# GLU contraction in two parts between the S5 steps, the last norm weight on ScalarE, S5 tables asked for eight slots later

## The chip, the cores and the metric

One core of one Trainium2 chip runs the whole kernel. The metric is the device time of one launch in microseconds; the kernel before takes 2509.47 us (median of three runs, 2509.09 to 2511.0).

## What is computed

One inference step of a two-layer decoder trunk, for a prompt of 256 tokens and for 8 samples of 4 new tokens each, with the same weights in float32. The first layer mixes with retention and a gated linear recurrence; the second with an S5 state space model whose output goes through a GELU and a GLU; each layer ends in a SwiGLU feed-forward network (FFN), and the trunk ends in a norm.

```python
D_MODEL = 2048
FFN_HIDDEN = 5632          # 44 tiles of 128
def odd_mixer(x, h0_re, h0_im, g, ..., w_glu, b_glu):
    u = rmsnorm(x, g)
    y, hr, hi = s5(u, h0_re, h0_im, ...)    # 128 groups of 16 channels, 64 complex states each
    y = jax.nn.gelu(y)
    z = y @ w_glu + b_glu                   # 2048 x 4096
    z1, z2 = jnp.split(z, 2, axis=-1)
    return z1 * jax.nn.sigmoid(z2), hr, hi
def swiglu(x, w_gu, w_down):
    g, u = jnp.split(x @ w_gu, 2, axis=-1)
    return (jax.nn.silu(g) * u) @ w_down
def trunk(x, ...):
    for layer in range(2):
        out = even_mixer(x, ...) if layer == 0 else odd_mixer(x, ...)
        x = x + out
        x = x + swiglu(rmsnorm(x, norm_ffn[layer]), ...)
    return rmsnorm(x, norm_final), states
```

## The kernel before

**Layout.** Channels lie on the 128 partitions (16 tiles of a 2048-wide vector, NT = 16) and the tokens on N = 288 columns: four S5 time steps of 72 columns, each 8 sample columns and 64 chunk columns. The trunk's value is `X` (128 x 16 x 288) in SBUF.

**Main matmuls.** A weight tile of 128 x 128 is used as a high and a low part, and so is the input: three matmuls of 288 columns for each tile, L314 (weight high, input high), L315 (weight high, input low) and L316 (weight low, input high). A *unit* is one tile of 128 output rows over a run of k-tiles. `halves_of` cuts a unit into two *slots* of weights, up to eight k-tiles or 1024 columns wide. Each slot goes through three steps: SyncE asks for its DMA (`raw`, L262, 512 KB, four buffers), ScalarE copies out the high part (`wh`, L268, four buffers), VectorE subtracts it for the low part (`wl`, in `tt` at L96, three buffers, and a fourth, `wlx`, from FFN0 on).

**What sets the order.** `run_prog` goes through the list `prog` item by item. Ahead of each item it issues DMAs for slots until four are ahead of the last subtracted one, copies until four are ahead of the last finished slot, and subtractions until three are (four while `hold` has an entry). `later(n, f)` puts `f` behind the n-th slot from now; `bgq` holds background work that runs behind slots. Each engine takes its instructions in the order in which they were issued, and SyncE's DMA queue (SPq) carries the weights, the S5 tables and the rows of X that S5 needs.

**The stages.** Even mixer (`w_in`, `w_out`); FFN0 (`w_gu`, `w_dn`, the 44 hidden tiles in thirds of 15, 15 and 14), in whose background `table_chunk` builds the S5 tables P, R, O and T into DRAM, through the DMA queue of GpSimd (POOL); `s5_open`, which asks for the S5 state `ss` and the first tables; `s5_core` and the S5 steps with the GLU among them; the other GLU units, in pairs of a z unit and a g unit for each of 16 output tiles; FFN1; `finish`, the last norm and the output.

**An S5 step** treats one tile of 128 channels: `st_a` multiplies the input by the norm and by table P (L1426, 32 small matmuls into `pp`); `st_b1` turns it by the table R on VectorE; `st_t` is a direct part with the table T (L1476, 16 small matmuls into `po`); `st_b2` runs two scans (L1451) and turns back, ending in the state `Hs`; `st_o` multiplies the state by the table O (L1486, 32 small matmuls into `po`); `st_d1`, `st_d1b`, `st_d2` and `st_d3` are the GELU and the split of its output. In a step j before, the GELU of groups j-2, j-3 and j-4 is under way (`st_d1(j-2)` to `st_d3(j-4)`), so that 20 steps are needed for 16 groups. Tables are double-buffered: `load("P", j + 2)`, `load("R", j + 1)`, `load("T", j + 1)` and `load("O", j)` at the head of `stage_a`. P, R and O are 512 KB each; T is put together by four strided DMAs into a tile that was zeroed once.

**GLU in the S5 steps.** Units 0 and 1 get one k-tile each, six matmuls in all, in each of the steps 4 to 19. Unit 2 gets its two halves behind steps 17 and 19. This is 144 of the GLU's 1536 matmuls; the other 29 units follow.

**The end.** Behind each FFN1 output tile `final_hook` squares it on ScalarE and adds it up on VectorE. `finish` sums over partitions with a matmul by ones, takes Ln and Exp on ScalarE for the reciprocal root and refines it, and then makes 16 products of 288 columns (`stt` at L105, X times weight times root), each with a DMA of its own.

Of the kernel before, what the change touches and what calls it, by code (L numbers as in the profile page):

```python
# [19 lines left out]
P = 128  # L20
# [26 lines left out]
def trunk_kernel(ctx: ExitStack, tc: tile.TileContext, ins, outs, upto=99, dbg=None):  # L47
# [6 lines left out]
    xgp = ctx.enter_context(tc.tile_pool(name="xgp", bufs=32))  # L54
# [16 lines left out]
    def xg_(dt=F32R):  # L71
        return xgp.tile([P, N], dt, tag="x", name=nm("xg"))

# [144 lines left out]
    def run_prog():  # L218
        ws, items, hold, fin_h = [], [], [], set()
        own = None  # L220
        lead = [u for u in prog if isinstance(u, Unit)][:4]
        for u in prog:
            if isinstance(u, Unit):
# [3 lines left out]
                for e in range(2):  # L227
                    for h in hs:
                        items.append((len(ws),) + h[e])
                        ws.append(h[e])  # L230
            elif isinstance(u, tuple):
                us, stages = u
                hs = [halves_of(x) for x in us]
                idx = {}
                for x, e in ((0, 0), (1, 0), (0, 1), (1, 1), (2, 0), (2, 1)):
                    idx[x, e] = len(ws)
                    ws.append(hs[x][e])
                items.append(lambda h=idx[2, 0]: hold.append(h))
                own = us[2]
                for a, segs, b, free in stages:  # L240
                    items.append(a)
                    for x, k0, k1 in segs:
                        items.append((idx[x, k0 >= hs[x][0][2]], us[x], k0, k1))
                    items.append(b)
                    if free:
                        items.append(hold.clear)
            else:
                items.append(u)
        accs = {}
        raws, whs, wls = {}, {}, {}  # L250
        n = len(ws)
        LH, RAW = 3, 4
        ring = S["ring"] = [wt.tile([P, 1024], F32R, name=f"wl{k}", bufs=1) for k in range(3)]
        free = S["free"] = list(ring)

        def size(i):
            return (ws[i][2] - ws[i][1]) * P

        def dma(i):
            u, a, b = ws[i]  # L260
            r = wt.tile([P, 1024], F32, tag="raw", name=nm("raw"), bufs=RAW)
            sp.dma_start(r[:, :size(i)], u.w[:, a * P:b * P])  # L262
            raws[i] = r

        def prep_h(i):
            w = size(i)
# [4 lines left out]
        def prep_l(i):  # L271
            w = size(i)
# [20 lines left out]
        for h in items:  # L293
            while True:
# [4 lines left out]
                if c[2] >= done + (4 if hold else 3) or c[2] >= n or c[2] in hold:  # L299
# [5 lines left out]
            i, u, a, b = h  # L305
            if a == u.k0:
                bank = mp_() if u in lead else S["bank"]() if u is own else psa.tile([P, 512], F32, tag="acc", name=nm("acc"))
                accs[id(u)] = (bank[:, :N], u.rhs())
            acc, rhs = accs[id(u)]
            wh, wl, w0 = whs[i], wls[i], ws[i][1]  # L310
# [1464 lines left out]
```

## Time and profile before

| | |
|---|---|
| runs | 2511.0, 2509.09, 2509.47 us (median 2509.47) |
| profiled execution | 2510.14 us, its span 2508.4 us |
| TensorE matmul (PE) | 2440.5 us busy, 97% |
| VectorE (DVE) | 1631.0 us busy, 65% |
| ScalarE (ACT) | 1126.3 us busy, 45% |
| GpSimd (POOL) | 113.6 us busy, 5% |
| DMA | 485.38 MB, 194 GB/s mean |
| chain that ended last | PE 93%, DVE 4%, DMA 2%, issue 1% |

Times are microseconds from the start of the span. The S5 steps lie from 1344 to 1455 us, the GLU's pairs from there to 1648 us, FFN1 to 2492 us. In the rows, a number in square brackets is the idle time of that engine just before the instruction, and behind the arrow stands what ended it; a line that is a helper's (L96 is every `tt`, L105 every `stt`) is told apart by the tile's name.

### The profile page before, as it was taken

Reading aid. Unit: us, or ns where it says so; the run is one execution under the profiler, and the core shown is the slowest. Engines: PE = TensorE matmul, PEld = TensorE weight load, DVE = VectorE, ACT = ScalarE, POOL = GpSimd, SP = SyncE. Lnnn points to the kernel's source line nnn. Section 1 sums busy time; section 2 is a strip of 40 time slices with the busy share of each in tenths; the row PEclk is TensorE's granted clock in tenths of the full one; section 3 lists DMA queues with packets and bytes.
Section 4 is the critical chain, followed back from the end, with each engine's and each line's share of the span. In section 5 each row is a group of like instructions: output and inputs, shape, how many; then the busy total and the mean of one; then the engine's idle time right before and its main releaser. Section 6 shows DMA issues by size and latency. Waiting matters only on the chain.

```text
span 2508.4 us, 49325 instructions
## 1 busy us (share of the span) xinstructions
PE 2440.5 (97%) x20090; PEld 2410.8 (96%) x20090; DVE 1631.0 (65%) x3011; ACT 1126.3 (45%) x1692; POOL 113.6 (5%) x221
## 2 busy tenths in 40 slices
PE   8999999999999999999997799999999999999997
PEld 8999999999999999999996689999999999999997
DVE  7767676667777887777847975555544555445554
ACT  6655554433455555455532444443333333333342
POOL 0111110000011011101100000000000000000000
PEclk9999999999999999999999899999999999999999
DMA  7555655555577778777788945555555555555553
GB/s 249 193 188 185 208 169 173 176 163 166 177 254 239 237 239 260 242 233 244 229 241 255 270 149 166 166 162 167 168 166 171 159 163 163 174 163 163 163 162 126
DMA packets 170371, 485.38 MB, mean 194 GB/s; under 512 B 35744, under 2 KB 52000, under 8 KB 170144
## 3 DMA queue, kind: packets, MB, share of 16 engines
q1 hardware_dynamic: 155792, 437.94, 55.6%
q0 software_dynamic: 12624, 42.95, 4.9%
q8 instruction: 158, 2.59, 0.4%
q10 hardware_dynamic: 1728, 1.33, 0.2%
q14 instruction: 69, 0.57, 0.1%
HBM read 440.77 MB, written 41.37 MB: 192 GB/s over the span
## 4 chain that ended last, share of the span: by engine, by line
PE 93%; DVE 4%; DMA 2%; issue 1%; ACT 0%; SPq 0%; DVEq 0%; POOL 0%; ACTq 0%; POOLq 0%
PE acc L314 30%; PE acc L316 29%; PE acc L315 29%; DVE w L96 2%; DVE w L1451 1%; DMA raw<-in_w_dn_dram 0%; PE mp L774 0%; DVE Hs L96 0%; PE mp L519 0%; DMA tab<-tabR 0%; DVE g L105 0%; PE mp L1297 0%; PE mp L315 0%; DMA tab<-tabP 0%; PE mp L316 0%
## 5 line engine op out<-in xcount | busy, mean ns | idle before, releaser
L314 PE MATMUL acc<-xg,wh 128*128 128x288 f32 x3520 | 1045.1, 297 | 0.0
L268 ACT ACTIVATE wh<-raw 128x1024 fp32r<-128x1024 f32 (+1 forms) x736 | 757.2, 1035 | 444.3 <-PE acc L315 297.3
L316 PE MATMUL acc<-xg,wl 128*128 128x288 f32 x2816 | 827.6, 294 | 0.8 <-DVE wl L96 0.8
L315 PE MATMUL acc<-xg,wh 128*128 128x288 f32 x2608 | 766.5, 294 | 1.6 <-DVE xg L105 1.6
L96 DVE TENSOR_TENSOR wl<-raw,wh 128x1024 fp32r<-128x1024 f32 (+1 forms) x585 | 692.8, 1197 | 37.3 <-ACT wh L268 29.6
L314 PEld LDWEIGHTS acc<-xg,wh 128*128 128x128 f32 x3520 | 660.3, 188 | 1.8 <-issue 0.8
L314 PE MATMUL acc<-ac,wh 128*128 128x288 f32 x2064 | 612.4, 297 | 4.5 <-ACT wh L268 2.2
L316 PEld LDWEIGHTS acc<-xg,wl 128*128 128x128 f32 x2816 | 529.7, 188 | 1.0 <-DVE wl L96 1.0
L315 PEld LDWEIGHTS acc<-xg,wh 128*128 128x128 f32 x2608 | 491.5, 188 | 2.5 <-DVE xg L105 2.0
L316 PE MATMUL acc<-ac,wl 128*128 128x288 f32 x1592 | 469.2, 295 | 1.3 <-DVE wl L96 1.3
L315 PE MATMUL acc<-ac,wh 128*128 128x288 f32 x1568 | 461.4, 294 | 0.0
L315 PE MATMUL acc<-x,wh 128*128 128x288 f32 x1408 | 415.4, 295 | 0.0
L314 PEld LDWEIGHTS acc<-ac,wh 128*128 128x128 f32 x2064 | 389.0, 188 | 7.0 <-ACT wh L268 2.5
L96 DVE TENSOR_TENSOR g<-acc,rstd 128x288 f32<-128x288 f32 x192 | 87.6, 457 | 341.4 <-PE acc L316 341.3
L316 PEld LDWEIGHTS acc<-ac,wl 128*128 128x128 f32 x1592 | 300.8, 189 | 1.5 <-DVE wl L96 1.5
L315 PEld LDWEIGHTS acc<-ac,wh 128*128 128x128 f32 x1568 | 295.9, 189 | 0.0
L315 PEld LDWEIGHTS acc<-x,wh 128*128 128x128 f32 x1408 | 264.2, 188 | 0.1
L316 PE MATMUL acc<-xg,wlx 128*128 128x288 f32 x704 | 206.8, 294 | 0.0
L96 DVE TENSOR_TENSOR X<-X,acc 128x288 f32<-128x288 f32 x112 | 50.9, 454 | 233.9 <-PE acc L316 233.6
L96 DVE TENSOR_TENSOR wlx<-raw,wh 128x1024 fp32r<-128x1024 f32 (+1 forms) x151 | 179.5, 1189 | 2.6 <-ACT wh L268 2.6
L191 ACT ACTIVATE ac<-g 128x288 fp32r<-128x288 f32 x98 | 43.5, 444 | 282.7 <-DVE g L96 282.7
L316 PE MATMUL acc<-ac,wlx 128*128 128x288 f32 x472 | 138.8, 294 | 0.0
(288 smaller groups left out, 2003.3 us busy)
## 6 DMA issues: line engine op xcount, KB each, us to landing
raw<-in_w_gu_dram SPq DMA_DIRECT2D x352, 512.0 KB, 4.6
raw<-in_w_dn_dram SPq DMA_DIRECT2D x128, 448.0 KB, 4.2
raw<-in_w_in_dram SPq DMA_DIRECT2D x96, 512.0 KB, 4.6
raw<-in_w_dn_dram SPq DMA_DIRECT2D x64, 512.0 KB, 3.7
raw<-in_w_glu_dram SPq DMA_DIRECT2D x64, 512.0 KB, 5.0
raw<-in_w_out_dram SPq DMA_DIRECT2D x32, 512.0 KB, 4.3
out_ret_s_dram<-s POOLq DMA_DIRECT2D x16, 512.0 KB, 5.6
pw<-tabW SPq DMA_DIRECT2D x128, 64.0 KB, 3.8
```

The source lines that it names most:

```text
L96: v.tensor_tensor(o, a, b, op=op)
L191: act.activation(h, x, AF.Copy, scale=scale)
L268: act.activation(wh[:, :w], raws[i][:, :w], AF.Copy)
L314: pe.matmul(acc, lhsT=wh[:, o:o + P], rhs=xh, start=(k == u.k0), stop=False)
L315: pe.matmul(acc, lhsT=wh[:, o:o + P], rhs=xl, start=False, stop=False)
L316: pe.matmul(acc, lhsT=wl[:, o:o + P], rhs=xh, start=False, stop=(k == u.k1 - 1))
L1451: v.tensor_tensor_scan(g[:, ri].rearrange("p q c -> p (q c)"), r4m, a[:, ri].rearrange("p q c -> p (q c)"), 0.0, op0=MUL, op1=ADD)
```

## The change

It has six parts.

1. The GLU is contracted in two parts. The first part of 28 of the 32 units (g0 to g11 over k-tiles 0 to 3, two units sharing a slot of 1024 columns; g12, g13 and z0 to z13 over k-tiles 0 to 5, in slots of 768) stands between the S5 steps: one k-tile of g0 and g1 each in the steps 2 to 5, two more units behind step 5, three behind steps 6 and 7, two behind each of the steps 8 to 16. These are 432 matmuls. ScalarE copies each part from PSUM to SBUF; the later unit over the remaining 10 or 12 k-tiles adds it (in the same `stt` for z, with one more `tt` for g). The unit 2 with its own PSUM bank and `hold` are gone. Units of the tiles 14 and 15 stay whole.
2. A step j now does the GELU of group j-1 from end to end, `st_o(j - 1)` stands at its head, and 17 steps do. The tables are asked for in other places of the step, P and O and T one step earlier.
3. T is put together in DRAM during FFN0 (`tabU` to `tabT`, zero-filled first, ten more POOL DMAs for each two groups) and loaded by one DMA of 256 KB.
4. `s5_open` runs eight slots later, and asks for `ss`, P0, R0, T0, P1, O0, R1, T1, O1 instead of `ss`, P0, P1, R0, T0.
5. S5's norm sum is four matmuls into 32 rows each, with one `ts` behind it instead of four; the matmuls that keep TensorE busy at S5's start are others.
6. The last norm's weight is multiplied into X on ScalarE behind each FFN1 output tile. `finish` takes the last tile's square into the matmul by ones directly, loads the ScalarE table ahead of time, and makes six products (576 to 1152 columns) with six DMAs.

```diff
@@ run_prog
-                us, stages = u
-                for x, e in ((0, 0), (1, 0), (0, 1), (1, 1), (2, 0), (2, 1)):
...
+                for pieces in u[0]:
+                    slot(*pieces)
+                items.extend(u[1])
...
-                if c[2] >= done + (4 if hold else 3) or c[2] >= n or c[2] in hold:
+                if c[2] >= done + 3 or c[2] >= n:
@@ final_hook
+    def last_hook(j):
+        if j == 0:
+            S["fb"] = cst.tile([P, N], F32, tag="nacc", name=nm("nacc"))
+        if j < NT - 1:
+            norm_acc(S["fb"], j, X[:, j, :])
+        else:
+            S["sq"] = g_()
+            act.activation(S["sq"], X[:, j, :], AF.Square)
+        act.activation(X[:, j, :], X[:, j, :], AF.Copy, scale=vec[:, V_FIN + j:V_FIN + j + 1])
@@ ffn, rest, table_chunk
-                call(lambda: act.activation(lnw, eps, AF.Ln))
+                call(lambda: act.preload_act_table_set("natural_log_exp_and_others"))
...
-        bgq.append(s5_open)
+        bgq.append(lambda: later(8, s5_open))
...
+            for jj in range(2):
+                pool.dma_start(tabT[2 * ch + jj].rearrange("p q c -> p (q c)"), ins["zero"])
...
-                pool.dma_start(tabT[j], T)
+                pool.dma_start(tabU[j], T)
...
+                for s in range(CH):
+                    pool.dma_start(tabT[j, 32 * s:32 * s + 32, :, 32 * s:], src[:, :, :P - 32 * s])
@@ s5_open
-        for k, j in (("P", 0), ("P", 1), ("R", 0), ("T", 0)):
+        for k, j in (("P", 0), ("R", 0), ("T", 0), ("P", 1), ("O", 0), ("R", 1), ("T", 1), ("O", 1)):
@@ s5_core
         def stage_a(j):
-            load("P", j + 2)
-            load("R", j + 1)
-            load("T", j + 1)
-            load("O", j)
-            if 0 <= j - 2 < NT:
-                st_d1(j - 2)
+            if j:
+                load("R", j + 1)
+                st_o(j - 1)
+                load("O", j + 1)
+                st_d1(j - 1)
             if j + 1 < NT:
                 st_a(j + 1)
...
+                load("P", j + 3)
             if j < NT:
                 st_b1(j)
                 st_t(j)
+                load("T", j + 2)
@@ glu
+        def first(key, w, k1, alloc):
+            def ev(ps):
+                part[key] = alloc()
+                act.activation(part[key], ps, AF.Copy)
+            cut[key] = k1
+            return Unit(w, 0, k1, lambda: xs["y"], ev)
+
+        g1 = [first(("g", j), ins["w_glu"][NT + j], 4 if j < 12 else 6, lambda: ac_(F32)) for j in range(NT - 2)]
+        g1 += [first(("z", j), ins["w_glu"][j], 6, lambda: xg_(F32)) for j in range(NT - 2)]
+        slots = [[(u, 0, 4) for u in g1[2 * i:2 * i + 2]] for i in range(6)] + [[(u, 0, 6)] for u in g1[12:]]
+        todo = deque(g1[2:])
+        seq = []
+        for t in range(NT + 1):
+            seq.append(lambda t=t: (S["a"](t), S["b"](t)))
+            if 2 <= t < 6:
+                seq += [(u, t - 2, t - 1) for u in g1[:2]]
+            for _ in range(0 if t < 5 else {6: 3, 7: 3}.get(t, 2)):
+                u = todo.popleft()
+                seq.append((u, 0, u.k1))
...
+                if ("g", j) in part:
+                    src = t_
+                    tt(t_, ps, part.pop(("g", j)), ADD)
...
-            segs = [(x, t - 4, t - 3) for x in range(2) if t >= 4]
@@ finish
-        norm_finish(acc, rstd["v"])
-        for j in range(NT):
-            y = g_()
-            stt(y, X[:, j, :], vec[:, V_FIN + j:V_FIN + j + 1], rstd["v"], MUL, MUL)
-            (sp if j % 2 else act).dma_start(outs["y"][:, j, :], y)
+        pe.matmul(ps[:, :N], lhsT=ones, rhs=S["fb"], start=True, stop=False)
+        pe.matmul(ps[:, :N], lhsT=ones, rhs=S["sq"], start=False, stop=True)
...
+        for q, a, b in ((sp, 0, 2), (act, 2, 5), (sp, 5, 9), (act, 9, 13), (sp, 13, 15), (act, 15, 16)):
+            y = X[:, a:b, :]
+            tt(y, y, r[:, None, :].to_broadcast([P, b - a, N]), MUL)
+            q.dma_start(outs["y"][:, a:b, :], y)
```

On VectorE, in one S5 step of the second half (`Hs` is the end of a step's state, the `w` rows the turns by table R, `g`, `xg` and `xl` the GELU). Before:

```order
L105 SCALAR_TENSOR_TENSOR g_16719<-g_16804,g_16718 128x288
L96 TENSOR_TENSOR Hs_16499<-w_16843,w_16904 128x8x64
L96 TENSOR_TENSOR xg_15937<-xg_15937,r4n 128x288
L96 TENSOR_TENSOR w_16949<-pp_16826,tab_16812 128x512
L96 TENSOR_TENSOR w_16950<-pp_16826,tab_16812 128x512
L105 SCALAR_TENSOR_TENSOR xg_16912<-g_16719,ac_16911 128x288
L96 TENSOR_TENSOR w_16949<-w_16949,w_16950 128x512
```

and with the change:

```order
L108 SCALAR_TENSOR_TENSOR g_17976<-g_18031,g_17975 128x288
L99 TENSOR_TENSOR Hs_16587<-w_18000,w_18029 128x8x64
L108 SCALAR_TENSOR_TENSOR xl_18037<-g_17976,ac_18036 128x288
L99 TENSOR_TENSOR wlx<-raw_17644,wh_17934 128x768
L99 TENSOR_TENSOR wl_119<-raw_17782,wh_18063 128x768
L99 TENSOR_TENSOR xg_16464<-xg_16464,r4n 128x288
L99 TENSOR_TENSOR w_18155<-pp_17981,tab_17939 128x512
L99 TENSOR_TENSOR w_18156<-pp_17981,tab_17939 128x512
L99 TENSOR_TENSOR w_18155<-w_18155,w_18156 128x512
```

Two subtractions of 768 columns have come in between one step's `Hs` and the next step's first turn, and the GELU's last product now stands behind `Hs` instead of among the turns.

On SyncE, the DMAs of one S5 step. Before:

```order
L1380 DMA tab_16708<-tabP 128x1024
L1380 DMA tab_16710<-tabR 128x1024
L1376 DMA T_1_15522<-tabT 32x4x128
L1376 DMA T_1_15522<-tabT 32x4x96
L1376 DMA T_1_15522<-tabT 32x4x64
L1376 DMA T_1_15522<-tabT 32x4x32
L1380 DMA tab_16716<-tabO 128x1024
```

and with the change:

```order
L261 DMA raw_17609<-in_w_glu_dram 128x768
L261 DMA raw_17644<-in_w_glu_dram 128x768
L1391 DMA tab_17646<-tabR 128x1024
L1391 DMA tab_17680<-tabO 128x1024
L1391 DMA tab_17705<-tabP 128x1024
L1391 DMA tab_17731<-tabT 128x512
```

Two weight loads of 384 KB now stand ahead of each step's table R, and T is one load.

On SyncE, where `s5_open` is issued, in the last third of FFN0's `w_dn` units (`ss` is the S5 state, `xd` a copy of X in DRAM). Before:

```order
L262 DMA raw_15490<-in_w_dn_dram 128x896
L1361 DMA xd<-X 128x288
L1386 DMA ss_15525<-in_state_ssm_dram 128x1024
L1380 DMA tab_15527<-tabP 128x1024
L1380 DMA tab_15529<-tabP 128x1024
L1380 DMA tab_15531<-tabR 128x1024
L1376 DMA T_0_15521<-tabT 32x4x128
L1376 DMA T_0_15521<-tabT 32x4x96
L1376 DMA T_0_15521<-tabT 32x4x64
L1376 DMA T_0_15521<-tabT 32x4x32
L262 DMA raw_15540<-in_w_dn_dram 128x896
```

and with the change:

```order
L261 DMA raw_15817<-in_w_dn_dram 128x896
L1394 DMA ss_15848<-in_state_ssm_dram 128x1024
L1391 DMA tab_15850<-tabP 128x1024
L1391 DMA tab_15852<-tabR 128x1024
L1391 DMA tab_15854<-tabT 128x512
L1391 DMA tab_15856<-tabP 128x1024
L1391 DMA tab_15858<-tabO 128x1024
L1391 DMA tab_15860<-tabR 128x1024
L1391 DMA tab_15862<-tabT 128x512
L1391 DMA tab_15864<-tabO 128x1024
L1377 DMA xd<-X 128x288
L261 DMA raw_15870<-in_w_dn_dram 128x896
```

The block is longer now, and stands eight slots later in the program.

## Rows read from the trace of the kernel before

**Rows 1.** Windows, by engine (busy us, instructions); then clock, DMA share, GB/s.
```profile
1400.00:1500.00 100.00, 81.69 (x1431) 76.41 (x1428) 82.20 (x143) 44.36 (x94) 5.63 (x10) 0.95 0.64 196
1500.00:1600.00 100.00, 100.00 (x759) 100.00 (x758) 53.91 (x71) 41.65 (x54) 0.00 (x0) 1.00 0.53 169
```
**Rows 2.** The last chain through one S5 step: start, us, what.
```profile
1404.59 0.68 DVE Hs L96
...
1405.63 1.20 DVE w L96 x2
1406.83 0.36 DVE xg L105
...
1407.84 1.27 DVE w L1451 x2
...
1410.95 0.68 DVE Hs L96
```
**Rows 3.** Timeline of VectorE: three ends of S5 steps, one wait for a table.
```profile
1350.85 0.69 DVE L96 TENSOR_TENSOR Hs<-w,w 128x512 f32<-128x512 f32 x1
1354.57 1.29 DVE L96 TENSOR_TENSOR w<-pp,tab 128x512 f32<-128x512 f32 x2 [2.66 <-DMA tab<-tabR]
1379.11 0.68 DVE L96 TENSOR_TENSOR Hs<-w,w 128x512 f32<-128x512 f32 x1
1448.78 0.68 DVE L96 TENSOR_TENSOR Hs<-w,w 128x512 f32<-128x512 f32 x1
```
**Rows 4.** Timeline of VectorE: subtractions for the low parts, two widths.
```profile
1322.54 2.09 DVE L96 TENSOR_TENSOR wl<-raw,wh 128x896 fp32r<-128x896 f32 x2
1333.64 2.35 DVE L96 TENSOR_TENSOR wl<-raw,wh 128x1024 fp32r<-128x1024 f32 x2
```
**Rows 5.** Timeline of TensorE in one S5 step.
```profile
1405.74 1.22 PE L1426 MATMUL pp<-xg,tab 128*64 128x72 f32 x32 [2.36 <-ACT g L1493]
1406.89 0.71 PE L1476 MATMUL po<-xg,T 128*32 128x72 f32 x32
1408.52 1.22 PE L1486 MATMUL po<-Hs,tab 128*32 128x72 f32 x64
```
**Rows 6.** Windows of two S5 steps each, columns as in rows 1.
```profile
1398.74:1411.47 12.73, 8.02 (x268) 7.03 (x268) 12.66 (x25) 4.89 (x16) 0.71 (x2) 1.00 0.94 275
1424.20:1436.94 12.74, 9.33 (x268) 8.29 (x268) 12.67 (x25) 4.90 (x16) 0.71 (x2) 0.87 0.85 239
```
**Rows 7.** Windows around the first table loads, columns as in rows 1.
```profile
1260.00:1270.00 10.00, 6.47 (x48) 6.00 (x47) 2.36 (x4) 2.29 (x4) 0.00 (x0) 1.00 0.99 314
1270.00:1280.00 10.00, 10.00 (x66) 10.00 (x65) 6.11 (x9) 4.90 (x7) 0.00 (x0) 0.83 0.93 268
```
**Rows 8.** DMA issues by tile in 1385 to 1440 us: count, size, us to landing.
```profile
tab<-tabR SPq DMA_DIRECT2D x9, 512.0 KB, 4.6
```
**Rows 9.** Timeline of TensorE: two places of the GLU and FFN1.
```profile
1461.70 0.40 PE L316 MATMUL pp<-ac,wl 128*128 128x288 f32 x1 [1.06 <-DVE wl L96]
1648.75 0.30 PE L315 MATMUL acc<-x,wh 128*128 128x288 f32 x1
```
**Rows 10.** Timelines of SyncE and TensorE where S5's first tables are asked for.
```profile
1250.35 0.38 SPq L1361 DMA_DIRECT2D xd<-X  x1
1255.68 0.33 SPq L1386 DMA_DIRECT2D ss<-in_state_ssm_dram  x1
1267.79 0.40 PE L314 MATMUL acc<-ac,wh 128*128 128x288 f32 x1 [2.23 <-ACT wh L268]
```
**Rows 11.** Timelines of VectorE and ScalarE behind the last main matmul; one window.
```profile
2492.96 0.46 DVE L96 TENSOR_TENSOR nacc<-nacc,g 128x288 f32<-128x288 f32 x1 [0.51 <-ACT g L173]
2494.78 1.28 ACT L183 ACT_TABLE_LOAD   x1
2498.03 6.96 DVE L105 SCALAR_TENSOR_TENSOR g<-X,vec,rstd 128x288 f32<-128x288 f32 x16
2500.00:2502.00 2.00, 0.00 (x0) 0.00 (x0) 2.00 (x6) 0.00 (x0) 0.00 (x0) 0.50 0.99 346
```

More of the change, by code (lines that the diff above doesn't have):

```diff
@@ L72, in xg_, with xl_ @@
         return xgp.tile([P, N], dt, tag="x", name=nm("xg"))
+    def xl_():
+        return xgp.tile([P, N], F32R, tag="xl", name=nm("xl"))
     def ac_(dt=F32R, w=N):
@@ L218, in run_prog, with slot @@
     def run_prog():
-        ws, items, hold, fin_h = [], [], [], set()
-        own = None
+        ws, items, where, left = [], [], {}, []
+        def slot(*pieces):
+            o = 0
+            for u, a, b in pieces:
+                for k in range(a, b):
+                    where[id(u), k] = (len(ws), a - o)
+                o += b - a
+            ws.append(pieces)
+            left.append(o)
         lead = [u for u in prog if isinstance(u, Unit)][:4]
@@ L321, in run_prog @@
                     u.evac(acc)
-            if b == ws[i][2]:
+            left[i] -= b - a
+            if left[i] == 0:
                 whs.pop(i)
                 free.append(wls.pop(i))
-                fin_h.add(i)
-                while done in fin_h:
-                    done += 1
+                assert i == done
+                done += 1
                 step[0] += 1
@@ L1463, in st_b2, with warm @@
             tabs.pop(("p", j))
-        def warm(ps, n):
-            for _ in range(n):
-                pe.matmul(ps, lhsT=ones, rhs=X[:, 0, :], start=True, stop=True, skip_group_check=True)
+            if j >= 1:
+                st_d3(j - 1)
+        def warm(ps, n, m, w=N):
+            xw = S["whs"][min(S["whs"])]
+            for k in range(n):
+                o = 32 * (k % 4) if m == 32 else 0
+                pe.matmul(ps[o:o + m, :w], lhsT=xw[:, 512:512 + m], rhs=xw[:, :w], start=True, stop=True,
+                          tile_position=(0, o), skip_group_check=True)
         def st_t(j):
@@ L1603, in glu @@
-        prog.append((us[:3], stages))
-        prog.extend(us[3:])
+                later(max(3 - j, 0), lambda: fin(j))
+            for key, w, e in ((("z", j), ins["w_glu"][j], e1), (("g", j), ins["w_glu"][NT + j], e2)):
+                k0 = cut.get(key, 0)
+                unit(w, k0, NT, lambda k0=k0: xs["y"][k0:], e)
+        for j in range(NT):
+            pair(j)
     def dump(name):
```

152 lines of the change are left out of this document (66 added, 86 removed).

## The prediction, made before the changed kernel was run

> **What bounds the kernel now.** I read windows of 100 us first: in the GLU's pairs TensorE is busy all the time at full clock while VectorE does 54 us of 100 and the DMA share is 0.53; in the window that holds the S5 steps TensorE is busy 82 of 100, and its instructions there are mostly the small S5 ones [rows 1]. So a matmul moved from the pairs into the S5 steps is a gain as long as a step does not get longer by as much. Then the chain that ended last, through one S5 step: every link is VectorE's, from one `Hs` at 1404.59 to the next at 1410.95, which is 6.36 us [rows 2]. From `Hs` of step 4 at 1379.11 to that of step 15 at 1448.78 there are eleven steps in 69.67 us, 6.33 each [rows 3]. In two such steps VectorE is busy 12.66 of 12.73 us and TensorE 8.02 [rows 6]: VectorE sets the step, and TensorE has about 2.4 us free in each. DMA is at a share of 0.94 there, with 275 GB/s [rows 6], so the queue is not idle either; this matters below.
>
> A main matmul's price: at 1461.70 the third matmul of the first k-tile in unit 2's second half runs, so 96 + 24 + 3 are done and 1413 of 1536 are left; FFN1's second matmul is at 1648.75 [rows 9]. That is 187.0 us for 1414 issues, 0.132 us each, the same as 100 us over 759 [rows 1].
>
> **Part 1 and 2, the GLU and the S5 steps.** What leaves the pairs: 432 matmuls stand among the steps after the change and 144 before, so 1104 are left behind the last step, 1104 x 0.132 = 145.9 us. What it costs is the length of the steps.
>
> VectorE. The step's own work stays: the same turns (1.20 twice), scans (1.27), `Hs` (0.68) and GELU pieces of about 0.36 [rows 2]; only their group is another. What is added are the subtractions of the weight slots. 1024 columns take 2.35 / 2 = 1.18 us, 896 take 1.05 [rows 4], so 0.13 less for each 128 columns and about 0.91 for 768. Three slots are ready before the first step, so the steps 6 to 15 hold about three of 1024 and fifteen of 768: 3 x 1.18 + 15 x 0.91 = 17.2 us. The steps before step 6 hold almost none. An ordinary filled step is then 6.35 + 2 x 0.91 = 8.2 us.
>
> TensorE. Small matmuls of a step: 1.2 (L1426), 0.7 (L1476) and 1.2 (L1486) [rows 5], with 36 x 0.132 = 4.75 for the two first parts: 7.9 us, just below 8.2. ScalarE has 4.89 us in two steps [rows 6] and gets two more copies of 768 columns and two evacuations a step, some 2.6 us by its own pace in [rows 1] (41.65 us over 54 instructions): 5 us, no bound.
>
> DMA. A step loads P, R and O (3 x 512 KB), T (256 KB) and two slots of 384 KB: 2.62 MB. In the fullest window the queue moved 314 GB/s at a share of 0.99 [rows 7]: 8.3 us, at 268 GB/s [rows 7] 9.8 us. So three resources stand within 5% of each other. I take 8.3, by the row with the share that such a step would have, which is 0.1 more than VectorE's. The Trainium skill ("DMA: Bandwidth & Descriptors", section Specifications) gives about 358 GB/s as one core's limit to HBM; by it a step's loads would take 7.3 us, VectorE would bound alone and the sum would be 1 us less; the row of this trace at a share of 0.99 is lower, and I go by the row.
>
> The path. `Hs` of step 0 is at 1350.85 [rows 3] and I leave it there; the new warm-up matmuls and the norm in one `ts` move it by under 1 us either way. Steps 0 to 4 took 28.3 us before, with a 2.66 us wait for table R [rows 3]; now R1, O0 and T1 are asked for ahead, so five steps of 6.4 give 1382.9 at step 5. Ten steps to step 15: 63.5 + 17.2 + 10 x 0.1 = 81.7, so 1464.6. Behind that one `st_o` (1.2), the GELU's chain of some seven pieces of 0.36 to 0.46 with waits, about 6 us, beside which the last first parts run (4.75): the pairs start again at 1471 to 1472, and FFN1 at 1472 + 145.9 = 1617.9, against 1648.6 now. I take **30 us**. From below: ten steps at 9.8 us give 15 us less, so 15. From above: no DMA term and a start at 1469 give 33.
>
> Inside the pairs a slot of 640 or 768 columns still holds 15 or 18 matmuls, 2.0 to 2.4 us, for a subtraction of 0.8 to 0.9 and a copy; VectorE at 54 of 100 [rows 1] covers the 14 extra additions of 0.46 [rows 11]. Cost nothing; if that cover failed it would be 14 x 0.46 = 6 us.
>
> **Part 3, T in DRAM.** Eighty more POOL DMAs in FFN0, 113.6 us of POOL in the whole kernel: another engine's queue, with a chunk's time of some tens of us to issue about ten. Nothing; were POOL late, the last chunk would delay `s5_open`, not the matmuls, and show as table waits in step 0.
>
> **Part 4, the first tables.** Now SyncE stands from 1250.7 to 1255.68 at `ss`, behind which the weight loads are queued; TensorE waits 2.23 us at 1267.79 [rows 10], and 48 + 66 matmuls run in 20 us where 151 would [rows 7]: 37 x 0.132 = 4.9 us lost. Eight slots later the wait of SyncE should be gone, since what `ss` waited for then lies 22 us back (8 x 21 x 0.132). But the block is ss, P, R and O twice and T twice, 4.06 MB, and the next weight load of 0.46 MB stands behind it: 4.5 MB at 314 GB/s is 14.4 us, with a landing of about 2 us 16.4. A load is asked for six slots ahead, 6 x 2.77 = 16.6 us, of which the copy and the subtraction take about 2 [rows 4]: about 2 us late, and the next loads late as well, as now. I estimate that 1 of the 4.9 us comes back; between -1 and 4.9.
>
> **Part 5** lies in the 1 us left at step 0.
>
> **Part 6, the end.** Behind the last matmul stand now the addition (0.46), the matmul by ones, Ln, a table load of 1.28 us, Exp, the refinement and 16 products in 6.96 us [rows 11]; then the output, 2.36 MB, at a share of 0.99 and 346 GB/s in the middle [rows 11], 6.8 us. The addition and the table load leave the chain, 1.74 us; the first product is 576 columns instead of 288, about 0.23 us more (half of 0.46). The products are done sooner (4608 columns at 0.60 us for 512 [rows 2] is 5.4 us), but the queue is what ends last, so its start counts: **1.5 us**. From 1.0 to 2.5. The 16 multiplications on ScalarE stand in FFN1, where it has over half its time free [rows 1]. The Trainium skill ("ScalarE: Activation LUTs", section What ACT_TABLE_LOAD costs) puts a switch at 2.66 us, 1.28 for the load as the row has it and 1.38 for draining; by it the end would come 1.4 us earlier still, but no row shows the second piece on the chain.
>
> **The sum.** 2508.4 - 30 - 1 - 1.5 = 2475.9 us of span; 1.74 us lie around it, and the median is 0.67 below the profiled execution: 2475.9 + 1.74 - 0.67 = 2477.
>
> **Rivals.** *The SPq queue sets the step.* R of two steps on is queued behind two weight loads, which wait for buffers that VectorE frees late in the step. It lands 4.6 us after its issue now [rows 8]; two loads of 384 KB at 314 GB/s add 2.5, 7.1 us, in a step of 8.2. At 268 GB/s, or with the issue 1 us later, VectorE waits at `st_b1` for R in every step, as it did once at 1354.57 [rows 3]. Steps of 9.5 to 10 us: 13 to 18 us less gain, so 2490 to 2495. For it: shares of 0.94 at 275 GB/s with far fewer bytes [rows 6]. Against: T's strided pieces are gone. Chance 0.24.
>
> *TensorE falls to its lower clock among the steps, and the kernel gets slower.* In two of the windows with equal work TensorE took 8.02 us at a granted 1.00 and 9.33 at 0.87, which is some time at 1.2 GHz instead of 2.4 [rows 6]; there it had been busy below three quarters of the time, and VectorE covered it. After the change nothing covers it: 7.9 us at full clock are 16 at the lower one, 10.8 at a mean of 0.73. The gain of 32.5 us is gone when eleven steps are longer by 2.95, thus at 11.1 us a step, a granted clock near 0.7. At 0.6 a step is 13.2 us, eleven times 5 more is 55, and the kernel ends at about 2532. Against it: TensorE gets nearly no idle time in these steps. The Trainium skill ("TensorE: Matmul & The Clock Gate", section A second HAM failure mode: psum-queue depth-cycling) tells of a kernel with short groups of matmuls in cycling PSUM banks whose clock swung; this change adds such groups, and the 0.87 row is a mild case of it. Chance 0.05.
>
> *The change doesn't do what it says at the small places:* the tables' block stalls as before or more, and the output queue ends as late. That is 2480, inside the forecast's own range.
>
> *Better:* SyncE's stall goes (4.9), the steps are VectorE's alone (33) and the end brings 2.5: 2508.4 - 40.4 + 1.07 = 2469.
>
> **How the numbers follow.** Forecast, 2469 to 2486 with 2477 as its time: 0.64. Steps held by the queue, 2486 to 2500: 0.24. Between these and no gain, 2500 to 2504: 0.03. Within 0.2%, which is 5 us and about what a measurement can tell from no change: 0.03. Slower: 0.05. Under 2469: 0.01. Faster is then 0.92. The range takes in both bounds of the step and most of the queue rival: 2466 to 2497.
>
> **What would show it.** `Hs` to `Hs` of 8.2 to 8.4 us in steps 8 to 14, subtractions of 0.91 among them and a DMA share near 1; fewer than 5% of VectorE's time there in waits for `tabR`. FFN1's first matmul near 1618. A granted clock of 0.9 or more in these steps. TensorE's wait in the last third of FFN0 of 3 to 4 us in all. The last matmul's end to the span's end 1.5 us shorter than now. Wrong if `Hs` to `Hs` is above 9.3 with waits for `tabR` or `tabP` (the queue), or if TensorE is busy through steps at 0.75 or less (the clock).

## The result, and the profile after

The changed kernel takes 2491.97 us (median of four runs, 2491.51 to 2493.15) against 2509.31 us before (2509.09 to 2511.0): a ratio of 0.9929, 95% interval 0.9918 to 0.9941, 17.3 us less. The forecast was 2477: the sign and the range (2466 to 2497) hold, the gain is a little over half of the 32.5 us forecast. The profiled executions differ by 18.7 us of span, 2508.4 to 2489.7.

Six places cut both spans into stretches, one of which is cut once more below. Where they lie after the change (timeline of VectorE; X is an output tile added into the trunk, the tile `mp` the norm that FFN1 waits for):

```profile
487.35 0.45 DVE L99 TENSOR_TENSOR X<-X,acc 128x288 f32<-128x288 f32 x1 [1.81 <-PE acc L317]
1345.22 0.45 DVE L99 TENSOR_TENSOR X<-X,acc 128x288 f32<-128x288 f32 x1 [1.85 <-PE acc L317]
1357.92 0.69 DVE L99 TENSOR_TENSOR Hs<-w,w 128x512 f32<-128x512 f32 x1
1472.45 0.69 DVE L99 TENSOR_TENSOR Hs<-w,w 128x512 f32<-128x512 f32 x1
1637.93 0.46 DVE L105 TENSOR_SCALAR g<-mp 128x288 f32<-128x288 f32 x1 [1.83 <-ACT g L184]
2474.82 0.45 DVE L99 TENSOR_TENSOR X<-X,acc 128x288 f32<-128x288 f32 x1 [4.14 <-PE acc L317]
```

The places of the kernel before that were not among the rows ahead of the prediction (its `Hs` stand in [rows 3]):

```profile
485.99 0.46 DVE L96 TENSOR_TENSOR X<-X,acc 128x288 f32<-128x288 f32 x1 [1.81 <-PE acc L316]
1337.85 0.45 DVE L96 TENSOR_TENSOR X<-X,acc 128x288 f32<-128x288 f32 x1 [1.86 <-PE acc L316]
1656.22 0.46 DVE L102 TENSOR_SCALAR g<-mp 128x288 f32<-128x288 f32 x1 [1.82 <-ACT g L181]
2492.00 0.45 DVE L96 TENSOR_TENSOR X<-X,acc 128x288 f32<-128x288 f32 x1 [4.11 <-PE acc L316]
```

FFN0 is cut once more, at the first output tile of its third down projection (1249.82 before, 1258.44 after). The forecast column goes by the times of the prediction's path, FFN1 at 1617.9; that is 30.7 us less, of which its sum took 30.

| stretch | before | after | difference | forecast |
|---|---|---|---|---|
| to the last X of the even mixer | 485.99 | 487.35 | +1.4 | 0 |
| FFN0 to its third down projection | 763.83 | 771.09 | +7.3 | 0 |
| third down projection (tables asked for) | 88.03 | 86.78 | -1.3 | -1 |
| to the first `Hs` | 13.00 | 12.70 | -0.3 | 0 |
| 15 S5 steps | 97.93 | 114.53 | +16.6 | +15.8 |
| last `Hs` to FFN1's norm | 207.44 | 165.48 | -42.0 | -46.5 |
| FFN1 | 835.78 | 836.89 | +1.1 | 0 |
| behind the last X | 16.40 | 14.88 | -1.5 | -1.5 |

So the steps came as worked out, and the tables and the end did within what one execution can tell. In the profiled executions of the experiments below that have the same code in a stretch, it spreads: to the last X of the even mixer 486.0 to 487.4 us, the third down projection 85.2 to 87.2, behind the last X 14.0 to 15.0. FFN0's 771.1 and FFN1's 836.9 come again within 0.2 us. Two things were not in the sum: 9.8 us in stages whose matmuls the change does not touch (1.4 of them hardly above the spread), and 4.5 us in the GLU's pairs.

**The steps.** One filled step on VectorE, what answers [rows 2], and below it windows of two steps, which answer [rows 6] (busy us of PE, PEld, DVE, ACT, POOL with instructions; clock, DMA share, GB/s):

```profile
1431.65 0.68 DVE L99 TENSOR_TENSOR Hs<-w,w 128x512 f32<-128x512 f32 x1
1432.25 0.45 DVE L108 SCALAR_TENSOR_TENSOR xl<-g,ac 128x288 fp32r<-128x288 f32 x1
1432.62 0.96 DVE L99 TENSOR_TENSOR wlx<-raw,wh 128x768 fp32r<-128x768 f32 x1
1433.50 0.95 DVE L99 TENSOR_TENSOR wl<-raw,wh 128x768 fp32r<-128x768 f32 x1
...
1439.89 0.68 DVE L99 TENSOR_TENSOR Hs<-w,w 128x512 f32<-128x512 f32 x1
```
```profile
1431.65:1448.12 16.47, 16.16 (x330) 15.05 (x330) 16.33 (x29) 9.37 (x22) 0.72 (x2) 1.00 0.95 317
1448.12:1464.59 16.47, 15.88 (x329) 14.77 (x328) 16.33 (x30) 9.36 (x22) 0.72 (x2) 1.00 0.89 290
```

A step is 8.24 us, where 8.2 to 8.3 was worked out: two subtractions have come in, VectorE is busy 16.33 of 16.47, TensorE 16 and at full clock, the queue at 0.89 to 0.95. From 1390 to 1470 this is the whole list of VectorE's waits (us in total, times, longest):

```profile
DVE w L99 <- DMA tab<-tabR: 0.3, 1, 0.3
```

So VectorE sets the step, with TensorE and the queue close behind. The chain that ended last, from 1395 to 1470, names landings of `tabO` and `tabR` for 37% of the time, but VectorE has no idle time before any instruction that the chain hangs on them.

**The pairs.** In the GLU's pairs, where TensorE had no idle time before [rows 1], it now has:

```profile
1500.00:1600.00 100.00, 98.16 (x723) 95.86 (x722) 63.78 (x110) 45.58 (x77) 0.00 (x0) 1.00 0.54 160
1510.00 0.41 PE L317 MATMUL acc<-ac,wl 128*128 128x288 f32 x1 [0.20 <-DVE wl L99]
1546.72 0.40 PE L317 MATMUL acc<-ac,wl 128*128 128x288 f32 x1 [0.19 <-DVE wl L99]
1565.66 0.40 PE L317 MATMUL acc<-ac,wl 128*128 128x288 f32 x1 [0.73 <-DVE wl L99]
```

The first line is the window, the others places on TensorE's timeline. From 1475 to the end of the pairs there are 24 gaps of more than 0.2 us between starts of matmuls, mostly two in a pair of units (0.41 and 0.24); beyond 0.132 each they sum to 5.1 us. What ends them is a low part, `wl`. Before the change there is no such gap behind the wait at 1461.70 [rows 9].

**The stages whose matmuls were not touched.** In FFN0's gate and up units TensorE is busy all the time in both kernels; yet it gets through fewer matmuls, which the windows show for the kernel before, the changed one, and the changed one again in FFN1:

```profile
500.00:600.00 100.00, 100.00 (x759) 100.00 (x758) 70.23 (x178) 38.47 (x48) 0.00 (x0) 1.00 0.52 165
500.00:600.00 100.00, 100.00 (x752) 100.00 (x751) 70.43 (x180) 38.65 (x48) 0.00 (x0) 1.00 0.52 163
1700.00:1800.00 100.00, 100.00 (x753) 100.00 (x752) 52.70 (x71) 38.14 (x47) 0.00 (x0) 1.00 0.53 168
```

The mean distance of two starts on the timeline has levels: 0.1322 us in the first and last third before and 0.1311 in the second, 0.1333 after in all three. That is 1440 x 1.1 ns, 1440 x 2.2 ns and 1344 x 1.1 ns = 6.2 us of FFN0's 7.3, all at a granted clock of 1.00. Another 0.8 lies in the second down projection, where 720 matmuls went from 0.1311 to 0.1322 too, with inputs that the new tag does not move. In FFN1's gate and up units both kernels have 0.1333; its 1.1 us lie in its down projections (0.1322, 0.1330 and 0.1319 before, 0.1325, 0.1337 and 0.1325 after).

### The profile page after: what moved, and what is told of

Its sections match the earlier page's. It is cut to its first block, busy times and chain, and to the rows that moved or that the text cites. A ratio compares the mean times of both kernels' runs of the same rounds, so it can differ in the third digit from the quotient of the medians.

```text
span 2489.7 us, 49585 instructions
## 1 busy us (share of the span) xinstructions
PE 2449.2 (98%) x20130; PEld 2419.2 (97%) x20130; DVE 1638.0 (66%) x3033; ACT 1145.3 (46%) x1756; POOL 154.2 (6%) x299
## 4 chain that ended last, share of the span: by engine, by line
PE 92%; DVE 4%; DMA 2%; ACT 1%; issue 1%; SPq 0%; DVEq 0%; ACTq 0%
PE acc L315 30%; PE acc L317 29%; PE acc L316 29%; DVE w L99 1%; DVE wl L99 1%; DMA tab<-tabO 1%; DMA raw<-in_w_glu_dram 1%; DMA raw<-in_w_in_dram 1%; DMA tab<-tabR 0%; DVE w L1459 0%; PE mp L775 0%; PE mp L520 0%; PE mp L1310 0%; ACT wh L268 0%; PE mp L723 0%
## 5 line engine op out<-in xcount | busy, mean ns | idle before, releaser
L315 PE MATMUL acc<-xg,wh 128*128 128x288 f32 x3520 | 1045.6, 297 | 0.0
L268 ACT ACTIVATE wh<-raw 128x1024 fp32r<-128x1024 f32 (+2 forms) x758 | 760.4, 1010 | 427.6 <-PE acc L316 262.7
L316 PE MATMUL acc<-xl,wh 128*128 128x288 f32 x2624 | 773.8, 295 | 0.0
L99 DVE TENSOR_TENSOR wl<-raw,wh 128x1024 fp32r<-128x1024 f32 (+3 forms) x601 | 697.5, 1173 | 24.6 <-ACT wh L268 16.3
L315 PEld LDWEIGHTS acc<-xg,wh 128*128 128x128 f32 x3520 | 659.6, 187 | 1.8 <-issue 0.8
L316 PEld LDWEIGHTS acc<-xl,wh 128*128 128x128 f32 x2624 | 493.0, 188 | 0.5
L317 PE MATMUL acc<-ac,wl 128*128 128x288 f32 x1626 | 480.8, 296 | 3.4 <-DVE wl L99 2.4
L317 PEld LDWEIGHTS acc<-ac,wl 128*128 128x128 f32 x1626 | 306.5, 189 | 5.9 <-DVE wl L99 5.9
L99 DVE TENSOR_TENSOR wlx<-raw,wh 128x1024 fp32r<-128x1024 f32 (+3 forms) x157 | 178.6, 1138 | 17.9 <-ACT wh L268 17.7
```

Of the source, the lines that this page charges most:

```text
L99: v.tensor_tensor(o, a, b, op=op)
L268: act.activation(wh[:, :w], raws[i][:, :w], AF.Copy)
L315: pe.matmul(acc, lhsT=wh[:, o:o + P], rhs=xh, start=(k == u.k0), stop=False)
L316: pe.matmul(acc, lhsT=wh[:, o:o + P], rhs=xl, start=False, stop=False)
L317: pe.matmul(acc, lhsT=wl[:, o:o + P], rhs=xh, start=False, stop=(k == u.k1 - 1))
```

## The experiments

Each is one edit of the kernel before or of the changed one, timed against the kernel before on the same chip; its median there was 2509.57, 2510.91 and 2509.7 us in three groups of four. Differences to the change are taken from its 2491.97; one of under 2 us tells nothing, as those medians alone are 1.6 apart with the 2509.31 from above.

### Where the low parts of the activations lie

The suspicion fell on a part of the diff that the prediction had passed over and that stands neither among the six parts of the change nor in the cuts of its diff: the low parts of the activations get buffers with a tag of their own. From that alone, a k-tile's high and low input lie 18432 bytes apart instead of 1152, and each group steps by one tile of 1152 bytes from k-tile to k-tile, where it stepped by two.

**Before, with separate buffers.**

```diff
-    xgp = ctx.enter_context(tc.tile_pool(name="xgp", bufs=32))
+    xgp = ctx.enter_context(tc.tile_pool(name="xgp", bufs=16))
+    def xl_():
+        return xgp.tile([P, N], F32R, tag="xl", name=nm("xl"))
...
-            l = xg_()
+            l = xl_()
```

> The kernel before with one thing of the change: the low parts of the activations get buffers of their own (16 and 16) instead of alternating with the high parts in one group of 32. Theory (placement): up to the last third of FFN0's down projection the changed kernel had fallen 8.6 us behind, with one main matmul every 0.1333 us in FFN0's gate and up units where the kernel before has 0.1322 (first and last third) and 0.1311 (second third); the two alternating inputs of a tile lie 1152 bytes apart before and 18432 apart after, so this edit alone brings 0.1333 there: 1440 x 1.1 ns + 1440 x 2.2 ns + 1344 x 1.1 ns = 6.2 us, and 1 to 3 us more in the projections, so 2516 to 2519 us. Rival (background): the eighty extra DMAs that put table T together slow TensorE, and this kernel, which has none of them, stays at 2509 us.

2517.51 us (2516.92 to 2518.43), ratio 1.0032, interval 1.002 to 1.0044: 7.9 us slower. The same window reads as in the changed kernel:

```profile
500.00:600.00 100.00, 100.00 (x752) 100.00 (x751) 70.78 (x180) 39.00 (x48) 0.00 (x0) 1.00 0.50 163
```

and the distance is 0.1333 in all three thirds. No DMA was added, so the background is out; up to FFN0's third down projection this edit alone loses 8.3 us, of the 8.6 that the changed kernel lost, and FFN0 up to there takes 771.1 us in both.

**After, with alternating places.**

```diff
     def xg_(dt=F32R):
-        return xgp.tile([P, N], dt, tag="x", name=nm("xg"))
+        cx[0] += 1
+        return xgp.tile([P, N], dt, tag=f"x{cx[0] % 16}", name=nm("xg"), bufs=1)
     def xl_():
-        return xgp.tile([P, N], F32R, tag="xl", name=nm("xl"))
+        cx[1] += 1
+        return xgp.tile([P, N], F32R, tag=f"l{cx[1] % 16}", name=nm("xl"), bufs=1)
```

> The changed kernel with the high and low parts of the activations in alternating places again (1152 bytes apart), the number of buffers as in the change. Placement: FFN0's gate and up units at 0.132 us a matmul or less, 6 to 8.6 us back, 2483 to 2486 us. Background: no difference, 2492 us.

2480.25 us (2479.04 to 2481.1), ratio 0.9883, interval 0.9868 to 0.9897: 11.7 us less than the change, more than expected. Its windows in FFN0 and FFN1:

```profile
500.00:600.00 100.00, 100.00 (x759) 100.00 (x758) 70.13 (x178) 38.42 (x47) 0.00 (x0) 1.00 0.52 165
1700.00:1800.00 100.00, 100.00 (x758) 100.00 (x757) 54.63 (x72) 39.15 (x48) 0.00 (x0) 1.00 0.51 165
```

0.1322 throughout FFN0, and in FFN1, where even the kernel before has 0.1333, 0.1322 in the first third and 0.1317 behind it, since its high parts now step by two tiles. FFN1 takes 830.75 us instead of 836.89; that is the half that I had not expected, and it is no loss undone, as the kernel before did not have it (835.78). Up to FFN0's third down projection 6.1 us of the 8.6 come back. The 0.1311 of the kernel before in its second third did not.

**After, alternating, low parts eleven tiles away from FFN0 on.** The places of the low parts are turned by five.

```diff
-        return xgp.tile([P, N], F32R, tag=f"l{cx[1] % 16}", name=nm("xl"), bufs=1)
+        return xgp.tile([P, N], F32R, tag=f"l{(cx[1] + 5 * ((cx[1] - 1) // 16)) % 16}", name=nm("xl"), bufs=1)
```

> As the kernel with alternating places, but from FFN0 on each low part lies 12672 bytes (11 tiles) from its high part instead of 1152, again not 18432. If it is the neighbouring place that counts, FFN0's gate and up units have 0.1333 us a matmul and the time is about 2490 us (the first projection alone keeps its gain); if it is the distance of 16 tiles that costs, they have 0.132 us or less and the time is 2483 to 2486 us.

2479.53 us (2478.35 to 2481.14), 0.1322 in FFN0: it is not the neighbouring place.

**After, separate groups, low parts in reverse and turned.** The other side of the same question: the distance varies, the step of each group stays one tile.

```diff
-        return xgp.tile([P, N], F32R, tag="xl", name=nm("xl"))
+        cx[0] += 1
+        return xgp.tile([P, N], F32R, tag=f"l{(cx[0] + 5 * ((cx[0] - 1) // 16)) % 16}", name=nm("xl"), bufs=1)
```

> The changed kernel with its two separate groups of buffers, but the low parts' places run the other way and, from FFN0 on, are turned by five: the distance between the high and the low part of a k-tile is no longer 18432 bytes and differs from k-tile to k-tile, while each group still steps by one tile of 1152 bytes from one k-tile to the next. Theory (step): in every stage seen so far with 0.1333 us a matmul both groups step by one tile (FFN1 of the kernel before too, where they lie 139520 bytes apart), and with 0.132 at least one steps by two; so 0.1333 stays, and 2490 to 2493 us. Rival (distance of 16 tiles): 0.132 in the projections and FFN0, 2483 to 2486 us.

2492.96 us (2490.41 to 2495.32), and 0.1333 as in the change:

```profile
500.00:600.00 100.00, 100.00 (x752) 100.00 (x751) 70.33 (x179) 38.55 (x48) 0.00 (x0) 1.00 0.53 162
```

So the distance of 16 tiles isn't it either. In the gate and up units of these kernels the distance of two starts is 0.1333 where both inputs step by one tile of 1152 bytes, and 0.1323 or less where at least one steps by two. Why TensorE does so no run shows.

### The waits in the GLU's pairs

**After, the next norm's work one slot later.**

```diff
-                later(max(3 - j, 0), lambda: fin(j))
+                later(max(3 - j, 1), lambda: fin(j))
```

> The changed kernel with the next norm's work behind a GLU output tile (split and square on ScalarE, addition on VectorE) put off by one more slot. In the GLU's pairs of the changed kernel TensorE waits about 0.4 us for a low part in each pair, 5.1 us in all, which it did not before. Theory (queued behind): the copies and subtractions of the next slots stand behind that work on ScalarE and VectorE; put off by a slot, they come first, and 3 to 4 us come back: 2488 to 2489 us. Rival (too short slots): with 15 to 18 matmuls a slot the look-ahead of three slots is too short whatever the order, and the time stays within 1 us of 2492.

2492.16 us (2490.64 to 2493.7): nothing. The gaps stand as before (24 of them, 5.5 us).

**After, three slots in a pair.** The k-tiles of z and g that remain are cut into three slots of six to eight that run across both units.

```diff
...
+            n = 2 * NT - z.k0 - g.k0
+            a = z.k0 + (n + 2) // 3
+            b = g.k0 + (n + 1) // 3 - (NT - a)
+            sl = [[(z, z.k0, a)], [(z, a, NT), (g, g.k0, b)], [(g, b, NT)]]
+            prog.append((sl, [p for s in sl for p in s]))
```

> The changed kernel with the GLU's remaining k-tiles of a pair (10 of z and 10 or 12 of g) cut into three slots of six to eight k-tiles that run across both units, instead of four slots of five or six. Theory (too short slots): with 18 to 24 matmuls a slot the low parts are ready again, the waits of 5.1 us in the pairs go, 2487 to 2488 us. Rival (the evacuation's longer chain, with the addition of the first part ahead of the tanh, holds the subtractions): the waits stay and the time is within 1 us of 2492.

2483.98 us (2481.41 to 2485.23), 8.0 us less than the change, 3 more than expected. The window of the pairs:

```profile
1500.00:1600.00 100.00, 100.00 (x754) 100.00 (x754) 66.14 (x104) 47.00 (x68) 0.00 (x0) 1.00 0.53 167
```

No gap is left in the pairs. From the last `Hs` to FFN1's norm it takes 161.04 us instead of 165.48, so 4.4 us are the slots'; 1.8 us lie ahead of the first `Hs`, in code that is the same, and the rest is the spread of the runs. The rival of this run (the longer chain behind a pair, with one more addition) falls: that chain stands here unchanged.

**After, without first parts of z.** The price of a moved matmul.

```diff
-        g1 += [first(("z", j), ins["w_glu"][j], 6, lambda: xg_(F32)) for j in range(NT - 2)]
...
```

> The changed kernel without the first parts of the 14 z units among the S5 steps: 252 matmuls go back into the GLU's pairs, and the steps from 10 on have no weight slots. By the prediction's prices the pairs get 252 x 0.132 = 33.3 us longer and the steps 14 x 0.91 = 12.7 us shorter: 20.6 us more, 2512 to 2513 us. If VectorE's step hides part of the subtractions, or the shorter slots' waits in the pairs go with the longer z units, less: 2506 to 2510 us.

2507.48 us (2505.86 to 2510.2), 15.5 us more than the change and 5 less than the two prices give. In the profiled executions 1.9 us lie ahead of the first `Hs`, in code that is the same. The 15 steps take 106.37 us, 8.2 less than with z (12.7 were worked out); from the last `Hs` to the norm it is 190.90, 25.4 more (33.3 worked out). The expectation put too much into both stretches. In the changed kernel one of the 14 subtractions and 41 of the 252 matmuls stand behind the last `Hs` already, and here three of the pairs' own subtractions, two of 1024 columns and one of 768, move up into the steps. That leaves 13 x 0.91 - 2 x 1.18 - 0.91 = 8.6 us for the steps and 211 x 0.132 = 27.9 for the stretch behind them. With whole z units no gap of the kind above is left in the pairs; so the 5.1 us of waits are part of the price of moving z in these slots. Against them stands a lower clock: behind the thinly filled last steps TensorE gets through fewer instructions in the 8 us from the last `Hs`, at a granted clock of 0.65 instead of 1.00 (first the changed kernel, then this one).

```profile
1472.45:1480.45 8.00, 8.00 (x116) 7.74 (x116) 5.94 (x12) 6.38 (x14) 0.91 (x2) 1.00 0.34 100
1462.34:1470.34 8.00, 7.22 (x93) 7.05 (x94) 3.65 (x9) 3.19 (x7) 0.91 (x2) 0.65 0.04 10
```

The 23 instructions are about 3 us at 0.132 each, and 27.9 - 5.1 + 3 = 25.8 where 25.4 were measured.

### What bounds a step

**After, without the low weight parts in the first parts.** Their third matmul is left out, and all but 128 columns of their subtractions; the loads stay.

```diff
-            w = size[i]
+            w = P if any(id(u) in S["nolo"] for u, _, _ in ws[i]) else size[i]
             wl = free.pop(0)
...
+                if id(u) in S["nolo"]:
+                    continue
                 pe.matmul(acc, lhsT=wl[:, o:o + P], rhs=xh, start=False, stop=(k == u.k1 - 1))
```

> The changed kernel without the low weight parts in the GLU's first parts: their third matmul (L317) is left out, and of their subtractions only 128 columns are made; all loads stay. VectorE loses about 1.5 us a step, TensorE 1.6 us, the queue nothing. Theory (VectorE sets the step of 8.23 us): the step falls until the next bound; the loads of 2.62 MB at the 317 to 364 GB/s that single steps of the changed kernel show take 7.2 to 8.3 us, so about 7.3 to 7.8, and 2486 to 2489 us. Rival (the SPq queue sets the step already): 8.1 to 8.3 us a step and 2491 to 2492 us.

2484.05 us (2483.41 to 2485.77), 2 us less than expected. The nine steps to the last take 69.17 us, 7.69 each, against 72.87, 8.10 each, with the change. The edit takes matmuls from TensorE too, so alone it does not tell the two apart; with VectorE's one wait of 0.3 us in the changed kernel it says that VectorE set the step, and that what comes next is close. A window of 8.24 us in such steps, VectorE's waits from 1395 to 1455 (us, times, longest), and one link of the chain of waits there (start, us, what):

```profile
1431.65:1439.89 8.24, 5.27 (x143) 4.70 (x143) 7.80 (x16) 4.86 (x12) 0.36 (x1) 1.00 0.99 351
...
DVE wl L99 <- ACT wh L268: 4.9, 5, 2.4
...
1452.23 7.11 DMA tab<-tabR
```

The queue is at a share of 0.99, VectorE now waits for copies on ScalarE that stand behind the evacuation of the first parts, and a landing of `tabR` of 7.11 us is on the chain. No single engine bounds the step any more; the queue of the prediction's rival is among those that do, 0.4 us a step behind VectorE.

### The first tables

**After, without the eight slots.**

```diff
-        bgq.append(lambda: later(8, s5_open))
+        bgq.append(s5_open)
```

> The changed kernel with S5's first tables asked for where the kernel before asks for them, without the eight slots. In the kernel before SyncE stands there about 5 us at the state's load and TensorE loses 4.9 us; in the changed kernel it lost 4.4 us at the later place. Theory: both losses stand at the old place, the wait of SyncE and the longer block, together 7 to 9 us instead of 4.4: 2495 to 2497 us. Rival (the block alone counts, SyncE's wait is hidden by the look-ahead): 2491 to 2492.5.

2499.0 us (2497.95 to 2503.2), 7.0 more than the change; 3 to 5 more were expected. Both losses stand in one place, SyncE's wait and then the block in the queue (timelines of SyncE and TensorE):

```profile
1258.16 0.44 SPq L1377 DMA_DIRECT2D xd<-X  x1
1264.74 0.33 SPq L1394 DMA_DIRECT2D ss<-in_state_ssm_dram  x1
1280.86 0.61 PE L315 MATMUL acc<-ac,wh 128*128 128x288 f32 x1 [7.48 <-ACT wh L268]
```

**After, the tables in two lots.**

```diff
-        for k, j in (("P", 0), ("R", 0), ("T", 0), ("P", 1), ("O", 0), ("R", 1), ("T", 1), ("O", 1)):
+        for k, j in (("P", 0), ("R", 0), ("T", 0), ("P", 1)):
             load(k, j)
+        def more():
+            for k, j in (("O", 0), ("R", 1), ("T", 1), ("O", 1)):
+                load(k, j)
+        later(8, more)
```

> The changed kernel with the first S5 tables asked for in two lots: state, P0, R0, T0 and P1 eight slots later as in the change, O0, R1, T1 and O1 another eight slots behind. In the changed kernel TensorE falls 4.4 us behind its own pace between 1288 and 1306 us, after the block of 4.06 MB. Theory (one block in the queue): two lots of 2.3 and 1.8 MB are each absorbed by the weights' look-ahead, the loss goes, 2487.5 to 2488.5 us. Rival (a second stall takes its place, or the S5 start waits for tables that now come late): 2490 to 2492 us.

2487.06 us (2485.85 to 2487.6), 4.9 less than the change. The window where the loss was, first in the changed kernel, then here:

```profile
1290.00:1310.00 20.00, 17.75 (x121) 17.28 (x120) 8.75 (x12) 7.66 (x10) 0.00 (x0) 0.91 0.95 305
1290.00:1310.00 20.00, 20.00 (x153) 20.00 (x152) 11.46 (x16) 9.07 (x12) 0.00 (x0) 1.00 0.97 315
```

32 matmuls more in 20 us, 4.2 us (in the changed kernel a part of it passes at a lower granted clock, 0.91 in the mean); the queue moves as much, but no weight stands behind all of it.

### The end alone, and the sum

**Before, with the change's end.** The kernel before with `last_hook` and `finish` of the changed one.

```diff
-    S["fb"] = {}
-    ffn(1, final_hook(None, S["fb"], "fin"))
+    ffn(1, last_hook)
```

> The kernel before with part 6 of the change alone (last norm weight on ScalarE, table loaded ahead, six wide products and six output DMAs). Theory of the prediction: the addition and the table load leave the chain and the output queue starts 1.5 us earlier, so the last addition into X to the end of the span is 14.9 us instead of 16.4, and the time is 2508 us; nothing else moves. Rival (wider first product and fewer, larger DMAs give it back): 16.4 us again and 2509.5.

2507.11 us (2506.65 to 2508.9), ratio 0.9988, interval 0.9979 to 0.9997; from the last X (2490.86) to the end of the span (2505.3) it is 14.4 us instead of 16.4. The other 1.1 us between the two profiled spans lie ahead of that, in code that is the same.

**After, with alternating places, two lots and three slots.**

> The changed kernel with three edits that each brought time alone: high and low parts of the activations in alternating places (-11.7 us), S5's first tables in two lots (-4.9 us), the GLU's remaining pairs in three slots (-8.0 us, of which 4.7 in the pairs' waits by the traces). If they do not overlap, 2492 - 11.7 - 4.9 - 4.7 to 8.0 = 2467 to 2471 us. If one cause lies behind two of them (the slower matmuls feed the stall or the waits), 2473 to 2478.

2469.0 us (2467.92 to 2472.32), ratio 0.9841, interval 0.9829 to 0.9854: 23 us less than the change, 40.7 less than before. The three causes are separate ones: each stretch is as short as where its edit stood alone, FFN0 up to its third down projection 766.55 us, that projection 82.38, from the last `Hs` to the norm 160.30. Only the sum of the three differences, 24.6, is not quite reached; of the 8.0 of the three slots 1.8 had come in code that is the same.

## Why the prediction was right and where it was not

**The matmul's price** (0.132 us, taken for every stage) was right in the GLU and wrong as a constant. The step that failed is one that isn't written: part 5 and the sum took every stage without a changed instruction at zero. The new tag for the low parts changes them all the same. Up to FFN0's third down projection 8.6 us were lost; the same edit on the kernel before loses 8.3 there (7.9 in the time), and alternating places give 6.1 back. FFN1's 1.1 us lie in its down projections; their cause stays open.

**The S5 steps**, the main term, held: +16.6 us for 15 steps where the sum had 15.8. VectorE bounds them, as its waits show: 0.3 us in 80. Leaving the subtractions out shortens them, and shows how close the next bound is.

The queue's term, 0.1 us a step, does not show in those waits. It came from 314 GB/s as the queue's most, and the changed kernel moves more in single windows (columns as in [rows 6]), one of them a step:

```profile
1280.00:1290.00 10.00, 10.00 (x78) 10.00 (x77) 5.62 (x8) 3.53 (x5) 0.00 (x0) 1.00 0.99 370
1415.65:1423.41 7.76, 7.50 (x162) 6.94 (x162) 7.39 (x14) 3.93 (x10) 0.36 (x1) 1.00 0.98 364
```

**The pairs**: "Cost nothing; if that cover failed it would be 14 x 0.46 = 6 us" named the right place and size, by the wrong part. It weighed VectorE's busy share and the additions; what failed was the look-ahead of three slots, once a slot holds 15 or 18 matmuls instead of 24. Three slots in a pair take the waits away, and the additions stay; so the length of the slots is shown as the cause, and the look-ahead is the reading of it from `run_prog`.

**The first tables**: -1.3 us where 1 was estimated; other executions with the same code there give -0.8 to -2.9. The block is 4.19 MB, not 4.06, which is 0.4 us more at the prediction's rate. The reason given, that the longer block stalls again about as much, is the one that the two runs show: without the delay 7.0 us worse, in two lots 4.9 better.

**T in DRAM**: nothing, as expected; the kernel before with the separate buffers has none of these DMAs and falls behind as far.

**The end**: -1.5 us as worked out (-2.0 in the kernel before with this end alone). From the last X to the first product it is 6.03 us before and 4.26 after, 1.77 less, against 1.74 for the addition and the table load as its row has it (timelines of ScalarE and VectorE, after):

```profile
2476.59 0.50 ACT L1651 ACTIVATE g<-mp,eps 128x288 f32<-128x288 f32 x1 [0.28 <-PE mp L1649]
2477.13 0.44 ACT L1653 ACTIVATE rstd<-g 128x288 f32<-128x288 f32 x1
2479.08 5.30 DVE L99 TENSOR_TENSOR X<-X,rstd 128x576 f32<-128x576 f32 x6
```

The figure of 2.66 us for a switch in the Trainium skill ("ScalarE: Activation LUTs", section What ACT_TABLE_LOAD costs) would have made 3.1 of it; the trace does not agree.

**The rivals.** The measured time is that of the queue rival (2490 to 2495), but not by its mechanism: steps are 8.24 us, not 9.5, and the waits for `tabR` are 0.3 us in all. That a range widened for the queue took in a loss in FFN0 is luck. Stalls of the rival's kind do come singly: with the same steps, one of 11.41 us stands in the run of reversed low parts, where VectorE waited 3.1 us for a copy on ScalarE and 0.8 for `tabR` in all the steps; why is not known. The lower clock did not come in the filled steps (1.00 granted); in the run without first parts of z, behind the last, thinly filled steps, matmuls follow each other at 0.24 us again. Of the Trainium skill's limit ("DMA: Bandwidth & Descriptors", section Specifications, about 358 GB/s) and the row's 314, two filled steps show 290 to 317, and 8.24 us of the run without low parts 351. The 364 and 370 above are over both figures, and the measurement decides.

## What to carry to other kernels

Filling a stage that another engine bounds pays by the price of the work that has to be prepared there, and that price could be read from rows of before to 5%. What a change of buffers does to stages that nobody edited has to be in the sum too: compare the places in memory, not only the instructions. Between executions a stretch of the same code spreads by 1 to 2 us here, so a term of that size needs more than one profile. Cutting work into shorter pieces shortens a look-ahead that is counted in pieces.

## What the hardware showed that was not expected

With all operands ready and the clock at its higher level, main matmuls of 288 columns came some 0.1311, 0.1322 or 0.1333 us apart in the gate and up units before and after, one level to a third. There the places of the inputs in SBUF choose between 0.1333 and less: 7.9 us when the slower ones were put into the kernel before, 11.7 us when they were taken out of both FFNs of the changed one. What made 0.1311 in one third of the kernel before, with the same places as in the others, and in the down projection behind it, stays open.
